# Turning the second layer's x through memory instead of on TensorE

## The chip, the cores and the metric

The kernel runs on one core of a Trainium2 chip. The time is device microseconds (us) of one execution; a comparison uses the median of several. The core's engines are named as in the profile: PE is TensorE (matmul), PEld its weight loads, DVE is VectorE, ACT is ScalarE, POOL is GpSimd, SP is SyncE, which here only issues DMAs. SBUF is the on-chip memory with 128 partitions; PSUM holds the sums of matmuls.

## The reference

Two layers of a decoder trunk, on 256 tokens of width 1024, all in float32. What matters here:

```python
for l in range(DEPTH):                       # DEPTH = 2
    h = rms_norm(x, norm_g[l])               # x * r, r = (mean(x*x) + eps) ** -0.5, times a gain per column
    proj = h @ w_in[l]                       # 1024 -> 10 groups of 512 columns
    q_a, k_a, v_a, q_h, f_h, i_h, q_m, z = jnp.split(proj, split_points, axis=-1)
    ...
    kv_m = rms_norm(mem, mem_norm_g[l]) @ w_mem_kv[l]
    k_m, v_m = jnp.split(kv_m, 2, axis=-1)   # keys are normalised again; cross-attention gives o_m
    ...
    y = jnp.concatenate([o_a, o_h, o_m], axis=-1) * jax.nn.silu(z)
    x = x + y @ w_out[l]
```

## The kernel before

All weights (60 chunks of 128 x 1024 per layer) pass through SBUF once. SyncE loads a chunk into one of four buffers (`wr`). A float32 product is made of three faster ones: each operand is split into a high part (a rounded copy) and a low part (the remainder). For a weight, ScalarE writes the high part (`wh`, line 214, or line 218 where a gain per row is multiplied in) and VectorE the low part (`wl`, lines 228 and 232); there are three buffers of each. TensorE then adds high x high, low x high and high x low into one of four PSUM accumulators of 512 columns (`acc`); four more PSUM tiles (`sd`) serve everything else.

The order of the layer: `group_kv` (line 301; chunks 0 to 7, keys and values of the memory, which don't depend on x), `group_a` twice (line 338; forget gate and query of HGRN2, chunks 8 to 15, which need the whole of hT), then the other groups, then `w_out_phase` (line 1247). Chunks are numbered through: the second layer begins with chunk 60, and its `group_kv` has chunks 60 to 67. `group_kv` takes chunks 0 to 5 with both halves (keys, values), then the key half of 6 and 7, then the value half of both; the key accumulators are copied out by VectorE and ScalarE (`kn`, lines 638 and 639), the value accumulators by `g_vm` (lines 679 and 680).

The work beside the matmuls is written as generators. Each `yield` ends a step, and `slot` (line 263) asks for the next chunks' splits and then lets every active generator do one step. A scheduler orders each engine's instructions by when they become ready and then by this program order; `in_turn` (line 139) fixes an order by hand, `keep_in_program_order` pins an instruction, and `tc.issue_after` puts one behind another on its queue.

`xs` holds x in SBUF, two tiles of 128 rows (tokens). The matmuls need the normalised x as columns: `hT`, 128 partitions x 8 blocks x (high, low) x 256 tokens. `g_norm` (line 468) makes it, in both layers alike:

- ScalarE squares x with a sum (line 473), VectorE makes the mean (line 477), GpSimd the power -0.5 (line 478): r, one number per row;
- VectorE multiplies x by r (line 481), 1024 columns, twice;
- TensorE transposes the 16 blocks of 128 x 128 into PSUM (line 489);
- for each of 8 blocks ScalarE writes the high part with the gain per column, now per partition (line 497), VectorE the low part (line 498).

In the second layer this runs while `group_kv` is on TensorE. x itself is finished in `w_out_phase`, at line 1305, in four additions of 512 columns.

Elsewhere the kernel already turns matrices without TensorE (`across`, line 88): VectorE transposes blocks of 32 x 32 in place (line 95), a DMA stores the result to memory (`there`, line 106), four DMAs load it back with the blocks in their new places (line 111). The keys do this on SyncE's queue, the HGRN output and the attention weights on GpSimd's.

Of the kernel before, what the change touches and what calls it, by code (L numbers as in the profile page):

```python
# [12 lines left out]
F32 = mybir.dt.float32  # L13
# [32 lines left out]
def hymba_kernel(ctx: ExitStack, tc: tile.TileContext, x, mem, mem_t, positions, w_in, w_out, w_mem_kv,  # L46
# [160 lines left out]
    def h_to(n):  # L207
        while st["h"] < min(n, len(chunks)):
            i = st["h"]
            whs[i] = sb.tile([128, 1024], F32R, name="wh", tag="wh", bufs=WH_BUFS)  # L210
            g = chunks[i][2]
            if g is None:
                with behind("ACT"):
                    nc.scalar.copy(whs[i], raws[i])  # L214
            else:
                for sl in parts(i):
                    with behind("ACT"):
                        nc.scalar.activation(whs[i][:, sl], raws[i][:, sl], AF.Copy, scale=gT[:, g:g + 1])  # L218
            st["h"] += 1

    def l_to(n):
# [79 lines left out]
    def group_kv(th, tl, km, vm):  # L301

        acc = [[acc_tile() for _ in range(2)] for _ in range(2)]

        def part(c, g):
            i = c + c0
            wH, wL = whs[i][:, g * 512:(g + 1) * 512], wls[i][:, g * 512:(g + 1) * 512]
            for t in range(2):
                ts = slice(t * 128, (t + 1) * 128)
                mm(acc[g][t], th[:, c, ts], wH, c == 0, False)  # L310
                mm(acc[g][t], tl[:, c, ts], wH, False, False)
                mm(acc[g][t], th[:, c, ts], wL, False, c == 7)

        def fin():
            i = st["c"]
            st["c"] += 1
            del whs[i], wls[i], raws[i]

        c0 = st["c"]
        for c in range(6):  # L320
            for g in range(2):
                part(c, g)
                if g == 1:
                    fin()
                slot(g == 1)
        for c in (6, 7):
            part(c, 0)
            if c == 7:
                spawn(km(acc[0]))
            slot(False)  # L330
        for c in (6, 7):
            part(c, 1)
            fin()
            if c == 7:
                spawn(vm(acc[1]))
            slot(True)
# [116 lines left out]
    def g_mem_r():  # L453
# [11 lines left out]
                                       in1=gT[:, GR_MK:GR_MK + 2], op0=OP.mult, op1=OP.mult)  # L465
        done.add("rm")

    def g_norm(l):
        yield from take("PTh", "PTl")
        xn = [sb.tile([128, D], F32, name="xn", tag=t, bufs=1) for t in ("PTh", "PTl")]  # L470
        ss = small("ssx", 2)
        for t in range(2):
            nc.scalar.activation(xn[t], xs[:, t], AF.Square, accum_out=ss[:, t:t + 1])
        yield 2
        ms = small("msx", 2)
        r = small("rx", 2)
        nc.vector.tensor_scalar(ms, ss, 1.0 / D, EPS, op0=OP.mult, op1=OP.add)
        nc.gpsimd.tensor_tensor(r, ms, pw[:, :2], op=OP.pow)
        yield
        for t in range(2):  # L480
            nc.vector.tensor_scalar(xn[t], xs[:, t], r[:, t:t + 1], None, op0=OP.mult)
        yield 3
        for kp in range(4):
            yield from room("sd")
            pt = side_tile()
            for j in range(2):
                k = kp * 2 + j
                for t in range(2):
                    ins = nc.tensor.transpose(pt[:, j * 256 + t * 128:j * 256 + (t + 1) * 128],  # L489
                                              xn[t][:, k * 128:(k + 1) * 128], ident)  # L490
                    if l == 0:
                        tc.keep_in_program_order(ins)
            for j in range(2):
                k = kp * 2 + j
                c = GR_NORM + 8 * l + k
                src = pt[:, j * 256:(j + 1) * 256]
                nc.scalar.activation(hTh[:, k], src, AF.Copy, scale=gT[:, c:c + 1])
                nc.vector.scalar_tensor_tensor(hTl[:, k], in0=src, scalar=gT[:, c:c + 1],
                                               in1=hTh[:, k].bitcast(F32), op0=OP.mult, op1=OP.subtract)
            rel()  # L500
            if kp % 2 == 1:
                yield
        rel("PTh")
        rel("PTl")
        done.add(f"hT{l}")
# [107 lines left out]
    for tag, n, bufs in (("PTh", 1792, 1), ("PTl", 1792, 1), ("hX", 512, 1), ("qk", 1024, 1), ("sq", 512, 2),  # L613
                         ("vmh", 1024, 1), ("vml", 1024, 1), ("kmh", 1024, 1), ("kml", 1024, 1), ("as", 512, 2),
                         ("al", 256, 2), ("hF", 1024, 1), ("sg", 512, 2), ("ih", 1024, 1),
                         *((f"y{c}{br}", 1024, 1) for br in (H_, A_, M_) for c in "hl"), ("hT1", 512, 1), ("blk", 1536, 1)):
        for _ in range(bufs):
            sb.tile([128, n], F32, name="place", tag=tag, bufs=bufs)

# [15 lines left out]
    def g_km(l, acc):  # L635
        ss = small("ssk", 8)
        kn = sb.tile([128, 2, 512], F32, name="kn", tag="qk", bufs=1)
        nc.vector.tensor_copy(kn[:, 0], acc[0])
        nc.scalar.copy(kn[:, 1], acc[1])  # L639
        yield  # L640
        for t in range(2):
            sumsq(ss[:, t * 4:t * 4 + 4], kn[:, t], 4)
        yield
        while "rm" not in done:
            yield
        ms = small("msk", 8)
        for t in range(2):
            nc.vector.tensor_scalar(ms[:, t * 4:t * 4 + 4], ss[:, t * 4:t * 4 + 4], rm2[:, t:t + 1], EPS,
                                    op0=OP.mult, op1=OP.add)
        r = small("rk", 8)  # L650
        nc.gpsimd.tensor_tensor(r, ms, pw[:, :8], op=OP.pow)
        for t in range(2):
            nc.gpsimd.tensor_scalar(r[:, t * 4:t * 4 + 4], r[:, t * 4:t * 4 + 4], rm[:, t:t + 1], None, op0=OP.mult)
        yield 3
        for t in range(2):
            nc.vector.tensor_tensor(heads(kn[:, t], 4), heads(kn[:, t], 4),
                                    r[:, t * 4:t * 4 + 4][:, :, None].to_broadcast([128, 4, 128]), op=OP.mult)
        yield 3
        kmh = sb.tile([128, 1024], F32R, name="kmh", tag="kmh", bufs=1)
        kt = sb.tile([128, 1024], F32, name="kml", tag="kml", bufs=1)  # L660
        kml = kt.bitcast(F32R)
        g = gkq[:, l:l + 1]
        yield from across(kt.rearrange("p (q r) -> p q r", q=4), kn.rearrange("p t s -> p (t s)"), 8)
        while f"ih{l}" not in done:
            yield
        yield 5
        tc.keep_in_program_order(nc.scalar.activation(kmh, kt, AF.Copy, scale=g))
        tc.keep_in_program_order(nc.vector.scalar_tensor_tensor(kml, in0=kt, scalar=g, in1=kmh.bitcast(F32),
                                                                op0=OP.mult, op1=OP.subtract))
        T["km"] = kmh, kml  # L670
        done.add(f"km{l}")

    def g_vm(l, acc):
        vmh = sb.tile([128, 2, 512], F32R, name="vmh", tag="vmh", bufs=1)
        vml = sb.tile([128, 2, 512], F32R, name="vml", tag="vml", bufs=1)
        while "rm" not in done:
            yield
        for t in range(2):
            nc.scalar.activation(vmh[:, t], acc[t], AF.Copy, scale=rm[:, t:t + 1])
            nc.vector.scalar_tensor_tensor(vml[:, t], in0=acc[t], scalar=rm[:, t:t + 1], in1=vmh[:, t].bitcast(F32),  # L680
                                           op0=OP.mult, op1=OP.subtract)
        T["vm"] = vmh, vml
        yield

# [87 lines left out]

    def y_tiles(br):
        if f"y{br}" not in T:
            T[f"y{br}"] = [sb.tile([128, 4, 256], F32R, name=f"y{c}{br}", tag=f"y{c}{br}", bufs=1) for c in "hl"]
        return T[f"y{br}"]

    def y_store(l, br, u, po):
# [468 lines left out]
    def w_out_phase(l):  # L1247
# [51 lines left out]
        for t in range(2):  # L1299
            for c in range(2):  # L1300
# [4 lines left out]
                nc.vector.tensor_tensor(xv, xv, acc[t][c], op=OP.add)  # L1305
                if last:
                    put(t, c * 512, c * 512 + (256 if split else 512))
                if split:
                    rest = side_tile()
                    both(t, c, 256, 256, last, rest)  # L1310
                    xv = xs[:, t, 768:]
                    nc.vector.tensor_tensor(xv, xv, rest[:, :256], op=OP.add)  # L1312
                    put(t, 768, 1024)
# [11 lines left out]
    for l in range(DEPTH):  # L1325
        group_kv(mTh, mTl, lambda a: g_km(l, a), lambda a: g_vm(l, a))
        need(f"hT{l}")
        group_a(hT, lambda h, a: g_f(l, h, a))
        group_a(hT, lambda h, a: g_q(l, h, a))
        for gen in (lambda l, a: g_qk(l, 1, a), g_ih, lambda l, a: g_qk(l, 0, a), g_zh, g_qm, g_va, A_, M_):  # L1330
            if gen in (A_, M_):
# [53 lines left out]
```

## Time and profile before

| what | value |
| --- | --- |
| median of three runs | 389.35 us (389.11 to 390.02) |
| the profiled execution's own time | 390.01 us |
| its span, first to last instruction | 388.2 us |
| PE / DVE / ACT / POOL busy | 382.4 / 320.5 / 247.6 / 85.3 us |
| second layer's `group_kv`, first to last matmul begun | 195.41 to 218.71 us |
| TensorE's transposes of x in it (16) | from 206.07 us, 1.91 us busy |
| first matmul with the second layer's hT | 219.09 us |

Times inside the execution are counted from the span's start. A line of a timeline has the start, the length, the engine, the line of the kernel, the operation, what it writes and reads, how many were merged, and in brackets the idle time before it with what ended it. A matmul's length is its way through a pipeline; the distance between starts is what it costs. In the lists of groups, the count is followed by the busy time and the mean of one in ns. A DMA line ends with the time from issue to landing.

### The profile page before, as it was taken

To read this page: it belongs to the slowest core of one execution; us is meant where nothing else is said; L and a number is where in the kernel's file an instruction comes from. 1 tells how busy PE (TensorE), PEld (TensorE's weight loads), DVE (VectorE), ACT (ScalarE), POOL (GpSimd) and SP (SyncE) were. 2 spreads that over 40 slices of the span, in tenths; PEclk is the share of its full clock that TensorE was granted. 3 is DMA by queue.
4 is the path that set the end of the run, shared out by engine and by line. 5 is a ranking of instruction groups with operands and counts; after the bars stand their busy time and mean duration, and the time that the engine had idled before them with its cause. 6 is when DMAs were issued, how large, how long until landed. Compare 5 with 4: busy or idle time off the path is not lost.

```text
span 388.2 us, 6790 instructions
## 1 busy us (share of the span) xinstructions
PE 382.4 (98%) x2455; PEld 319.2 (82%) x2455; DVE 320.5 (83%) x621; ACT 247.6 (64%) x414; POOL 85.3 (22%) x129
## 2 busy tenths in 40 slices
PE   7999999999999999999999999999999999999996
PEld 5888888788888888788888888888888889887885
DVE  4789899999659999958577689899696699998663
ACT  5988755567768849754375756445765984785540
POOL 3004400434202623400000040014062054252000
PEclk9999999999999999999999999999999999999999
DMA  8985595439534999985465568736866179999512
GB/s 266 417 307 181 188 320 181 162 113 312 177 108 140 289 289 365 286 258 176 155 210 164 175 206 234 254 110 180 252 191 195 54 255 275 322 335 280 175 39 108
DMA packets 26241, 84.48 MB, mean 218 GB/s; under 512 B 3552, under 2 KB 5984, under 8 KB 26208
## 3 DMA queue, kind: packets, MB, share of 16 engines
q1 hardware_dynamic: 22304, 71.31, 55.7%
q0 software_dynamic: 3616, 12.59, 10.4%
q8 instruction: 19, 0.31, 0.3%
q10 hardware_dynamic: 288, 0.15, 0.1%
q14 instruction: 14, 0.11, 0.1%
HBM read 74.60 MB, written 9.44 MB: 216 GB/s over the span
## 4 chain that ended last, share of the span: by engine, by line
PE 97%; DMA 1%; DVE 0%; SPq 0%; ACT 0%; issue 0%; DVEq 0%
PE acc L276 69%; PE acc L1261 17%; PE sd L276 6%; PE sd L280 4%; DMA wr<-in_w_mem_kv_dram 1%; PE sd L489 1%; PE sd L1017 0%; PE sd L1147 0%; SPq L178 0%; ACT wh L218 0%; DVE xs L1305 0%; DVE xs L1312 0%; DVEq L1312 0%
## 5 line engine op out<-in xcount | busy, mean ns | idle before, releaser
L214 ACT CAST wh<-wr 128x1024 fp32r<-128x1024 f32 x96 | 100.8, 1051 | 68.1 <-PE acc L276 46.8
L228 DVE TENSOR_TENSOR wl<-wr,wh 128x1024 fp32r<-128x1024 f32 x96 | 116.8, 1217 | 26.1 <-ACT wh L214 26.0
L276 PE MATMUL acc<-wh,hT 128*128 128x512 f32 x384 | 122.9, 394 | 0.0
L276 PEld LDWEIGHTS acc<-wh,hT 128*128 128x128 f32 x384 | 71.5, 188 | 15.8 <-issue 0.7
L276 PE MATMUL acc<-wl,hT 128*128 128x512 f32 x192 | 75.6, 394 | 0.0
L276 PE MATMUL acc<-hT,wh 128*128 128x512 f32 x256 | 64.8, 392 | 0.0
L276 PEld LDWEIGHTS acc<-hT,wh 128*128 128x128 f32 x256 | 46.0, 189 | 8.4 <-ACT kn L639 0.4
L276 PEld LDWEIGHTS acc<-wl,hT 128*128 128x128 f32 x192 | 36.1, 188 | 7.3
L1261 PE MATMUL acc<-wh,yl 128*128 128x512 f32 (+1 forms) x96 | 37.2, 387 | 0.0
L1261 PE MATMUL acc<-wl,yh 128*128 128x512 f32 (+1 forms) x96 | 37.2, 387 | 0.0
L232 DVE SCALAR_TENSOR_TENSOR wl<-wr,gT,wh 128x1024 fp32r<-128x1024 f32 (+1 forms) x29 | 31.2, 1096 | 7.1 <-ACT wh L218 7.0
L276 PEld LDWEIGHTS acc<-hT,wl 128*128 128x128 f32 x256 | 34.9, 190 | 2.5
L218 ACT ACTIVATE wh<-wr,gT 128x1024 fp32r<-128x1024 f32 (+1 forms) x29 | 28.3, 1000 | 12.4 <-PE acc L1261 4.1
L276 PE MATMUL acc<-hT,wl 128*128 128x256 f32 x256 | 35.7, 282 | 0.0
L1261 PE MATMUL acc<-wh,yh 128*128 128x512 f32 (+1 forms) x96 | 33.1, 392 | 0.0
L276 PE MATMUL acc<-wh,mTh 128*128 128x512 f32 x64 | 25.3, 399 | 1.2 <-ACT wh L218 0.9
L276 PE MATMUL acc<-wh,mTl 128*128 128x512 f32 x64 | 24.8, 390 | 0.0
L982 POOL TENSOR_TENSOR rka<-msa,pw 128x8 f32<-128x8 f32 x4 | 9.9, 2475 | 58.2 <-DVE msa L981 58.2
L1068 ACT ACTIVATE P<-P,nba,rq 128x128 f32<-128x128 f32 (+1 forms) x32 | 17.1, 537 | 8.3 <-DVE nba L1062 8.3
L1261 PEld LDWEIGHTS acc<-wh,yh 128*128 128x128 f32 x96 | 18.0, 188 | 4.1 <-issue 0.7
L1261 PEld LDWEIGHTS acc<-wh,yl 128*128 128x128 f32 x96 | 18.0, 188 | 3.7
L1261 PEld LDWEIGHTS acc<-wl,yh 128*128 128x128 f32 x96 | 18.0, 188 | 3.5
(219 smaller groups left out, 589.2 us busy)
## 6 DMA issues: line engine op xcount, KB each, us to landing
wr<-in_w_in_dram SPq DMA_DIRECT2D x80, 512.0 KB, 3.7
wr<-in_w_out_dram SPq DMA_DIRECT2D x24, 512.0 KB, 6.0
wr<-in_w_mem_kv_dram SPq DMA_DIRECT2D x15, 512.0 KB, 4.4
there<-blk POOLq DMA_DIRECT2D x4, 768.0 KB, 5.5
PT<-there POOLq DMA_DIRECT2D x16, 192.0 KB, 4.8
there<-blk POOLq DMA_DIRECT2D x6, 512.0 KB, 5.3
there<-blk SPq DMA_DIRECT2D x4, 512.0 KB, 2.9
P<-there POOLq DMA_DIRECT2D x16, 128.0 KB, 6.9
```

What stands on the lines that cost most here:

```text
L214: nc.scalar.copy(whs[i], raws[i])
L218: nc.scalar.activation(whs[i][:, sl], raws[i][:, sl], AF.Copy, scale=gT[:, g:g + 1])
L228: N["wl", i] = nc.vector.tensor_tensor(wls[i], raws[i], whs[i].bitcast(F32), op=OP.subtract)
L232: ins = nc.vector.scalar_tensor_tensor(wls[i][:, sl], in0=raws[i][:, sl], scalar=gT[:, g:g + 1], in1=whs[i][:, sl].bitcast(F32), op0=OP.mu ...
L276: nc.tensor.matmul(o, lhsT=a, rhs=b, start=s, stop=e)
L280: tc.keep_in_program_order(nc.tensor.matmul(o, lhsT=a, rhs=b, start=s, stop=e))
L489: ins = nc.tensor.transpose(pt[:, j * 256 + t * 128:j * 256 + (t + 1) * 128], xn[t][:, k * 128:(k + 1) * 128], ident)
L982: nc.gpsimd.tensor_tensor(r[:, t8], ms[:, t8], pw[:, :8], op=OP.pow)
L1068: nc.scalar.activation(P[:, i, kc[t]], P[:, i, kc[t]], AF.Exp, bias=nb[:, c:c + 1], scale=rq[:, r:r + 1], accum_out=sm[:, c:c + 1])
L1261: ins = nc.tensor.matmul(a, lhsT=y, rhs=wt[:, cs], start=n == (0 if to is None else nk - 2) and j == 0, stop=n == nk - 1 and j == 2)
```

## The change

In the second layer the 16 transposes on TensorE, the multiplication by r beforehand (line 481) and the 16 splits out of PSUM (lines 497 and 498) go. The first layer stays as it is. Instead:

- As soon as a half of x (128 rows) is finished, VectorE turns its 32 x 32 blocks (`x_turn`), not yet normalised, and GpSimd's queue stores it. Both stores are ahead of the loads: four loads for each half are placed behind the power instruction (`T["xr"]`) and behind each other, and bring x back as columns into `xT`, a tile that takes the room of the HGRN branch's y.
- The factor r, one number per row, has become one per column. VectorE copies it over 128 columns (`rc`), and two matmuls with the identity spread it into PSUM (`rb`).
- VectorE multiplies each of 8 column blocks in place by its gain (per partition) and by `rb` (256 columns each). Then ScalarE copies the high parts, four blocks at once, and VectorE subtracts for the low parts (1024 columns each).
- The order on VectorE and on ScalarE around this, from chunk 66 to chunk 70, is fixed with `in_turn`, and the matmuls of chunks 6 and 7 of the second layer's `group_kv` are pinned to program order.

```diff
+        def part(c, g, pinned=False):
...
+                for a, b in ((th, wH), (tl, wH), (th, wL)):
+                    ins = nc.tensor.matmul(acc[g][t], lhsT=a[:, c, ts], rhs=b, start=c == 0 and (a, b) == (th, wH),
+                                           stop=c == 7 and (a, b) == (th, wL))
+                    if pinned:
+                        tc.keep_in_program_order(ins)
...
-            part(c, 0)
+            part(c, 0, c0 > 0)
...
-            part(c, 1)
+            part(c, 1, c0 > 0)
...
+    def x_turned():
+        return sb.tile([128, 8, 256], F32, name="xT", tag=f"y{H_}", bufs=1)
+
+    def x_turn(t):
+        blk = sb.tile([128, 4, 256], F32, name="blk", tag=f"hq{t}", bufs=1)
+        N["xt", t] = nc.vector.transpose(blk.rearrange("p c (n i) -> p c n i", n=8),
+                                         xs[:, t].rearrange("p (n c i) -> p c n i", n=8, c=4))
+        yield
+        there = away.tile([4, 32, 4, 256], F32, name="there", tag="there", bufs=5)
+        T[f"there{t}"] = there
+        T[f"xstore{t}"] = nc.gpsimd.dma_start(there.rearrange("q j c r -> (q j) c r"), blk)
+        done.add(f"xstore{t}")
+        while "xr1" not in done:
+            yield
+        yield 2 + 2 * t
+        for c in range(4):
+            with tc.issue_after(T["xr"].ins):
+                ins = nc.gpsimd.dma_start(T["xT"][c * 32:c * 32 + 32, 4 * t:4 * t + 4],
+                                          there[:, :, c].rearrange("q j r -> j q r"))
+        T["xr"] = ins
+        done.add(f"x{t}moved")
+
+    def g_columns(l, r):
+        xT = T["xT"].rearrange("p q (k i) -> p q k i", i=32)
+        rc = sb.tile([128, 2, 128], F32, name="rc", tag="sq", bufs=2)
+        nc.vector.tensor_copy(rc, r[:, :, None].to_broadcast([128, 2, 128]))
+        yield from reach(l, 4)
+        yield from room("sd")
+        rb = side_tile()
+        for t in range(2):
+            mm_row(rb[:, t * 128:(t + 1) * 128], rc[:, t], ident)
+        rb3 = rb[:, :256].rearrange("p (q i) -> p q i", i=32)
+        while not {"x0moved", "x1moved"} <= done:
+            yield
+        for k in range(8):
+            c = GR_NORM + 8 * l + k
+            N["xT", k] = nc.vector.scalar_tensor_tensor(xT[:, :, k], in0=xT[:, :, k], scalar=gT[:, c:c + 1], in1=rb3,
+                                                        op0=OP.mult, op1=OP.mult)
+        rel()
+        for q in range(2):
+            ks = slice(4 * q, 4 * q + 4)
+            src = xT[:, :, ks].rearrange("p q k i -> p k q i")
+            hi, lo = (a[:, ks].rearrange("p k (q i) -> p k q i", i=32) for a in (hTh, hTl))
+            N["hTh", q] = nc.scalar.copy(hi, src)
+            N["hTl", q] = nc.vector.tensor_tensor(lo, src, hi.bitcast(F32), op=OP.subtract)
+        done.add(f"hT{l}")
...
-        nc.gpsimd.tensor_tensor(r, ms, pw[:, :2], op=OP.pow)
-        yield
+        T["xr"] = nc.gpsimd.tensor_tensor(r, ms, pw[:, :2], op=OP.pow)
+        done.add(f"xr{l}")
+        yield
+        if l:
+            rel("PTh")
+            rel("PTl")
+            yield from g_columns(l, r)
+            return
...
+                elif c:
+                    if t == 0:
+                        T["xT"] = x_turned()
+                    spawn(x_turn(t))
...
+        if l:
+            c = 60 * l
+            in_turn(("wl", c + 6), *(("xT", k) for k in range(4)), ("wl", c + 7), ("hTl", 0),
+                    *(("xT", k) for k in range(4, 8)), ("hTl", 1), ("kn", 0), ("wl", c + 8), ("wl", c + 9), ("vml", 0),
+                    ("vml", 1), ("wl", c + 10))
+            in_turn(("wh", c + 6), ("wh", c + 7), ("hTh", 0), ("wh", c + 8), ("hTh", 1), ("kn", 1), ("wh", c + 9), ("vmh", 0),
+                    ("vmh", 1), ("wh", c + 10))
```

The rest of the diff gives names to the instructions that the two lists use, and puts the two halves of the HGRN branch's y into one tile.

More of the change, by code (lines that the diff above doesn't have):

```diff
@@ L213, in h_to @@
                 with behind("ACT"):
-                    nc.scalar.copy(whs[i], raws[i])
+                    N["wh", i] = nc.scalar.copy(whs[i], raws[i])
             else:
@@ L217, in h_to @@
                     with behind("ACT"):
-                        nc.scalar.activation(whs[i][:, sl], raws[i][:, sl], AF.Copy, scale=gT[:, g:g + 1])
+                        N["wh", i] = nc.scalar.activation(whs[i][:, sl], raws[i][:, sl], AF.Copy, scale=gT[:, g:g + 1])
             st["h"] += 1
@@ L303, in group_kv @@
         acc = [[acc_tile() for _ in range(2)] for _ in range(2)]
-        def part(c, g):
+        def part(c, g, pinned=False):
             i = c + c0
@@ L309, in part @@
                 ts = slice(t * 128, (t + 1) * 128)
-                mm(acc[g][t], th[:, c, ts], wH, c == 0, False)
-                mm(acc[g][t], tl[:, c, ts], wH, False, False)
-                mm(acc[g][t], th[:, c, ts], wL, False, c == 7)
+                for a, b in ((th, wH), (tl, wH), (th, wL)):
[3 more added lines that the diff above has]
+                        tc.keep_in_program_order(ins)
         def fin():
@@ L615, in hymba_kernel @@
                          ("al", 256, 2), ("hF", 1024, 1), ("sg", 512, 2), ("ih", 1024, 1),
-                         *((f"y{c}{br}", 1024, 1) for br in (H_, A_, M_) for c in "hl"), ("hT1", 512, 1), ("blk", 1536, 1)):
+                         (f"y{H_}", 2048, 1), *((f"y{c}{br}", 1024, 1) for br in (A_, M_) for c in "hl"), ("hT1", 512, 1), ("blk", 1536, 1)):
         for _ in range(bufs):
@@ L637, in g_km @@
         kn = sb.tile([128, 2, 512], F32, name="kn", tag="qk", bufs=1)
-        nc.vector.tensor_copy(kn[:, 0], acc[0])
-        nc.scalar.copy(kn[:, 1], acc[1])
+        N["kn", 0] = nc.vector.tensor_copy(kn[:, 0], acc[0])
+        N["kn", 1] = nc.scalar.copy(kn[:, 1], acc[1])
         yield
@@ L678, in g_vm @@
         for t in range(2):
-            nc.scalar.activation(vmh[:, t], acc[t], AF.Copy, scale=rm[:, t:t + 1])
-            nc.vector.scalar_tensor_tensor(vml[:, t], in0=acc[t], scalar=rm[:, t:t + 1], in1=vmh[:, t].bitcast(F32),
-                                           op0=OP.mult, op1=OP.subtract)
+            N["vmh", t] = nc.scalar.activation(vmh[:, t], acc[t], AF.Copy, scale=rm[:, t:t + 1])
+            N["vml", t] = nc.vector.scalar_tensor_tensor(vml[:, t], in0=acc[t], scalar=rm[:, t:t + 1],
+                                                         in1=vmh[:, t].bitcast(F32), op0=OP.mult, op1=OP.subtract)
         T["vm"] = vmh, vml
@@ L774, in y_tiles @@
         if f"y{br}" not in T:
-            T[f"y{br}"] = [sb.tile([128, 4, 256], F32R, name=f"y{c}{br}", tag=f"y{c}{br}", bufs=1) for c in "hl"]
+            if br == H_:
+                y = sb.tile([128, 2, 4, 256], F32R, name=f"y{br}", tag=f"y{br}", bufs=1)
+                T[f"y{br}"] = [y[:, 0], y[:, 1]]
+            else:
+                T[f"y{br}"] = [sb.tile([128, 4, 256], F32R, name=f"y{c}{br}", tag=f"y{c}{br}", bufs=1) for c in "hl"]
         return T[f"y{br}"]
```

## The prediction

> **What bounds the kernel now.** I read the busy table and the chain of waits first.
>
> ```profile
> span 388.2 us, 6790 instructions
> PE 382.4 (98%) x2455; PEld 319.2 (82%) x2455; DVE 320.5 (83%) x621; ACT 247.6 (64%) x414; POOL 85.3 (22%) x129
> PEclk9999999999999999999999999999999999999999
> PE 97%; DMA 1%; DVE 0%; SPq 0%; ACT 0%; issue 0%; DVEq 0%
> ```
>
> TensorE is the bound: 97% of the chain is TensorE behind TensorE, at full granted clock in every slice. So an instruction taken off TensorE is worth its own time, and a hole torn into TensorE costs its own length. Next, the chain in order of time where the second layer begins (columns: start, length, what):
>
> ```profile
> 195.57 10.66 PE acc L276 x47
> 206.23 1.75 PE sd L489 x16
> 207.97 42.39 PE acc L276 x215
> ```
>
> The 16 transposes of x (L489) sit in the middle of the memory-key/value phase, with no idle time on either side: 1.75 us that nothing hides. One 512-column matmul takes 10.66/47 = 0.227 us. The TensorE timeline has the end of that phase and the beginning of the next, the four forget-gate groups that need the whole of hT:
>
> ```profile
> 195.41 0.39 PE L276 MATMUL acc<-wh,mTh 128*128 128x512 f32 x1
> ...
> 218.71 0.39 PE L276 MATMUL acc<-wl,mTh 128*128 128x512 f32 x1
> 219.09 2.14 PE L276 MATMUL acc<-hT,wh 128*128 128x512 f32 x8
> ```
>
> 219.09 us is the time to beat: whatever brings the first hT matmul forward shortens the kernel by as much, because the engine is full from there on.
>
> **What goes from TensorE.** 1.75 us of transposes. In their place come two 128x128 products with the identity that spread the row factors over columns. The nearest row of that shape:
>
> ```profile
> 111.27 1.27 PE L276 MATMUL sd<-ih,hST 128*128 128x128 f32 x10
> 112.38 0.39 PE L276 MATMUL sd<-ih,hX 128*128 128x128 f32 x2
> ```
>
> Ten of them pass between 111.27 and 112.38, 0.11 us each, so two cost 0.22 us. The phase has 96 matmuls (8 chunks, 2 halves, 2 row tiles, 3 products): 195.41 + 96 x 0.227 + 0.22 = 217.4 us is when TensorE could begin on hT. Against 219.09 that is a gain of at most 1.7 us. (Some 0.15 us of it is the wait before 219.09, while an accumulator of the phase was copied out.)
>
> **What must be ready by 217.4.** The new path is turn, store, load, scale, split. I follow the second half of x, the last to be ready. The VectorE timeline:
>
> ```profile
> 192.60 1.28 DVE L1305 TENSOR_TENSOR xs<-xs,acc 128x512 f32<-128x512 f32 x2
> ...
> 195.61 0.69 DVE L1305 TENSOR_TENSOR xs<-xs,acc 128x512 f32<-128x512 f32 x1 [0.67 <-PE acc L1261]
> 196.21 2.47 DVE L232 SCALAR_TENSOR_TENSOR wl<-wr,gT,wh 128x1024 fp32r<-128x1024 f32 x2
> ...
> 200.54 1.41 DVE L481 TENSOR_SCALAR xn<-xs,rx 128x1024 f32<-128x1024 f32 x2
> ```
>
> The residual is whole at 196.3. A turn of 1024 columns takes 1.24 us:
>
> ```profile
> L95 DVE STREAM_TRANSPOSE blk<-zh 128x1024 f32<-128x1024 f32 x2 | 2.5, 1238 | 0.0
> ```
>
> The turn ends at 197.5 if it goes straight behind the addition, at 200.2 if both weight remainders (2.47 us) go first and the first half's turn has pushed the additions back by 0.2 to 0.3. I take 198.75, one remainder ahead, because the second one's operand comes from ScalarE only at 197.17 (194.98 + 2.19), so it need not win the engine:
>
> ```profile
> 194.98 2.19 ACT L218 ACTIVATE wh<-wr,gT 128x1024 fp32r<-128x1024 f32 x2
> ```
>
> The first half is whole at 193.88; its turn and store fall into 193.9 to 196 and end nothing. GpSimd's queue is empty there: its only work between the layers is the row-factor power, which the loads are put behind and which the stores pass.
>
> ```profile
> 198.85 0.72 POOL L478 TENSOR_TENSOR rx<-msx,pw 128x2 f32<-128x2 f32 x1 [35.83 <-DVE msx L477]
> 225.49 2.54 POOL L651 TENSOR_TENSOR rk<-msk,pw 128x8 f32<-128x8 f32 x1 [25.91 <-DVE msk L648]
> ```
>
> Behind the loads, which hold that queue while a store lands, the next instruction is at 225.49: nobody waits for it.
>
> The trip through memory has two kinds of precedent: the key turns on SyncE's queue, and the HGRN output on GpSimd's.
>
> ```profile
> 46.74 0.33 SPq L106 DMA_DIRECT2D there<-blk  x1
> 49.64 1.76 SPq L111 DMA_DIRECT2D kml<-there  x4
> 133.20 0.60 POOL L106 DMA_DIRECT2D there<-blk  x1
> 138.98 2.23 POOL L111 DMA_DIRECT2D zh<-there  x4 [4.79 <-DMA there<-blk]
> zh<-there POOLq DMA_DIRECT2D x8, 128.0 KB, 5.1
> DMA to landing us min/median/max: 3.6/5.1/6.4
> kT<-there SPq DMA_DIRECT2D x8, 128.0 KB, 4.8
> ```
>
> Store to first load is 2.9 us in the one, 5.8 in the other; the fourth load is issued 1.7 us later (3 x 2.23/4), and a load lands after about 5 (3.6 to 6.4 for the HGRN output, least and most). Which store is nearer? The windows (length, busy times of PE, PEld, DVE, ACT, POOL, clock, DMA share, GB/s):
>
> ```profile
> 196.00:200.00 4.00, 4.00 (x20) 3.30 (x19) 3.43 (x5) 3.30 (x5) 0.72 (x1) 1.00 0.37 103
> 200.00:204.00 4.00, 4.00 (x19) 3.32 (x18) 3.14 (x4) 2.29 (x2) 0.00 (x0) 1.00 0.78 290
> 204.00:208.00 4.00, 4.00 (x27) 3.57 (x26) 1.86 (x3) 2.24 (x5) 0.00 (x0) 1.00 0.83 255
> 133.00:139.00 6.00, 6.00 (x40) 5.49 (x40) 6.00 (x14) 1.74 (x4) 1.17 (x4) 1.00 0.94 282
> ```
>
> At 196 to 200 the DMA engines are 37% busy, at 133 to 139 they are 94% busy. The store begins in the first kind of weather, so I take 2.9 plus 0.3 for GpSimd's slower issue (0.60 against 0.33) = 3.2, and for the loads 5.1 plus 0.4 because eight go out, not four, and the weights keep the engines at about 0.8. The last piece of x then lands at 198.75 + 3.2 + 1.7 + 5.5 = 209.15. Bounds: 197.5 + 2.9 + 1.7 + 3.6 = 205.7 and 200.2 + 5.8 + 1.7 + 6.4 = 214.1.
>
> The Trainium skill ("DMA: Bandwidth & Descriptors", section on the anatomy of a DMA on the GpSimd path) gives about 2.0 us plus bytes over 436 GB/s, which makes 3.2 us for a 512 KB store and 2.3 for a 128 KB load. The store rows agree with that; the load rows (4.8 and 5.1) do not, and by the page's figure x would land near 206 and the full 1.7 us be gained.
>
> **From landing to the first matmul.** The order is now written out. Prices:
>
> ```profile
> 209.80 2.04 DVE L498 SCALAR_TENSOR_TENSOR hT<-sd,gT,hT 128x256 fp32r<-128x256 f32 x5
> 211.98 1.28 DVE L232 SCALAR_TENSOR_TENSOR wl<-wr,gT,wh 128x1024 fp32r<-128x1024 f32 x1
> 214.60 1.23 DVE L228 TENSOR_TENSOR wl<-wr,wh 128x1024 fp32r<-128x1024 f32 x1 [1.33 <-ACT wh L214]
> 218.46 0.68 DVE L638 COPY kn<-acc 128x512 f32<-128x512 f32 x1
> 213.51 1.05 ACT L214 CAST wh<-wr 128x1024 fp32r<-128x1024 f32 x1 [1.56 <-PE acc L276]
> 218.45 0.59 ACT L639 COPY kn<-acc 128x512 f32<-128x512 f32 x1 [1.17 <-PE acc L276]
> ```
>
> On VectorE: four column scalings at 2.04/5 = 0.41 (1.64), the remainder of chunk 67 (1.24), the low half of hT's first four (1.22), four more scalings (1.64), then a wait for ScalarE's cast of those (1.05, nothing else in between, since the order is fixed), the second low half (1.22), the copy of the key accumulator (0.68). That is 8.7 us from landing until VectorE has released its accumulator and TensorE can go on; if TensorE needs the ScalarE-copied accumulator first it starts sooner, but the remainder of chunk 68 then comes late, and I count 8.2. I take 8.5, plus 0.2 for hand-overs: 209.15 + 8.7 = 217.85. The gain is 219.09 - 217.85 = **1.24 us**. The profiled execution took 390.01 us (388.2 of span), so its like would be 388.8; from the median of 389.35, which lies 0.66 below the profiled one, it is 388.1.
>
> Break-even follows: hT's path must start by 219.09 - 8.7 = 210.4. Each microsecond later than 208.7 costs a microsecond.
>
> **Waits that the fixed order adds.** Behind the first scaling on VectorE are queued the remainder of chunk 67 and everything to chunk 70. Chunk 67's is needed at 195.41 + 13 x 6 x 0.227 + 0.22 + 0.45 = 213.8, by the third matmul of its first part, which is now pinned; it is done at 209.15 + 2.9 = 212.05, so 1.7 us of cover, gone if x lands after 210.9. VectorE gains two turns, a broadcast copy (0.4, as one scaling) and two 1024-column subtractions (2.48 + 0.4 + 2.44) against 1.41 removed: 3.9 us more, and by the windows it idles 0.6 + 0.9 + 2.1 us of 196 to 208. This holds, but with no room. ScalarE trades eight 256-column casts for two of 1024, which is less.
>
> **Rivals.** (a) *The wait eats the gain*: x lands near 210.4 and hT is as late as before, 389.4. For it: the two unknowns that I took near their good ends (the turn's place, the load's time) have that sum well inside their bounds. Against: a DMA system that is idle in half of 196 to 200.
>
> (b) *Slower: the second store is late and the loads crowd the weights.* The turn waits for both remainders (200.2), the store takes 4.5, halfway between the two precedents, the loads 1.7 + 5.5: landing at 211.9, first hT matmul at 220.6, 1.5 us later than before: 390.9; with the whole 5.8 it is 392.2. It decides from 210.4 on, and is measurable from 211.2. For it: from 200 the engines are at 0.8 already and 1.5 MB of x are added; the stage at 133 to 139 shows what 94% does. The Trainium skill says so too ("DMA: Bandwidth & Descriptors", section on issuing engines not being separate queues): another issuing engine brings no bandwidth, all run on the same 16. Against: weights are fetched ahead, so their slack can give way first.
>
> (c) *Slower, weights late*: x delays two chunks of the phase itself.
>
> ```profile
> wr<-in_w_mem_kv_dram SPq DMA_DIRECT2D x15, 512.0 KB, 4.4
> 202.86 1.15 ACT L218 ACTIVATE wh<-wr,gT 128x1024 fp32r<-128x1024 f32 x1 [1.57 <-PE acc L276]
> ```
>
> A load of 4.4 us stretched to 7 is 2.6 late; ScalarE has 1.57 us to spare before a cast, so about 1 us of hole is left each time, 2.1 for two: 390.2. Against: ScalarE waits there for TensorE, not for a load.
>
> (d) *The change does not do what it says*: TensorE would have waited in those 1.75 us anyway. The chain shows no idle there; it gives 389.4.
>
> **The numbers.** Forecast 388.1 with 0.50 (its own range 387.6 to 388.6); (a) 0.22, (b) 0.20, (c) 0.06, (d) 0.02. About 0.2%, 0.78 us, is what a measurement can tell from none. Faster by more: 0.50; same: 0.22 + 0.02 = 0.24; slower: 0.20 + 0.06 = 0.26. The range reaches from 387.5 (all 1.7 us and a little) to 391.2, past the centre of (b); somewhat under half of (b) and a few per cent below are left out.
>
> **What would show it.** In the profile of after: no L489 transposes near 206; the second half's turn ending near 198.75; the last load of x landing near 209; the first hT matmul near 217.9, and TensorE without a hole before it. A hole of over 1.2 us in front of that matmul, released by VectorE (hT or the copy of the key accumulator), would be (a) or (b); one inside the phase, at chunk 67's remainder or a weight, (b) or (c).

## The result, and the profile after

The change makes the kernel slower: 395.04 us (392.98 to 396.60, five runs) against 389.35, ratio 1.0141 with a 95% interval of 1.0116 to 1.0165. The profiled execution is the slowest of the five, 396.60 us, 6.6 above the profiled one of before.

The page of the changed kernel, its head:

```profile
span 394.8 us, 6779 instructions
PE 383.5 (97%) x2443; PEld 319.9 (81%) x2443; DVE 322.9 (82%) x624; ACT 246.6 (62%) x408; POOL 88.5 (22%) x139
PEclk9999999999999999999999699999999999999999
PE 89%; DMA 6%; DVE 3%; issue 1%; ACT 0%; POOL 0%; SPq 0%; DVEq 0%; ACTq 0%
```

TensorE still reads 97% busy, which tells nothing. The two other lines tell it: one slice of the granted clock (the share of TensorE's full clock, in tenths) has a 6, and the chain, which was TensorE for 97%, now runs for 6% of the span through DMAs. The chain in order of time:

```profile
196.92 1.25 DVE blk L475
198.17 0.39 issue
198.56 7.28 DMA there<-blk
205.84 0.39 issue
...
207.90 8.79 DMA xT<-there
216.96 0.18 DVE xT L506
...
218.61 1.21 DVE wl L232
219.87 6.22 PE acc L311 x16
226.08 33.19 PE acc L276 x176
```

The second half of x is turned where the prediction had it, then takes 7.28 us to be stored and 8.79 for the last load, and VectorE begins the scaling at 216.96. The TensorE timeline has what that does:

```profile
194.89 0.39 PE L311 MATMUL acc<-wh,mTh 128*128 128x512 f32 x1
...
213.25 0.39 PE L311 MATMUL acc<-wh,mTl 128*128 128x512 f32 x1
219.87 0.79 PE L311 MATMUL acc<-wl,mTh 128*128 128x512 f32 x1 [6.22 <-DVE wl L232]
220.46 0.63 PE L311 MATMUL acc<-wh,mTh 128*128 128x512 f32 x1
220.88 0.63 PE L311 MATMUL acc<-wh,mTl 128*128 128x512 f32 x1
...
225.92 3.79 PE L276 MATMUL acc<-hT,wh 128*128 128x512 f32 x16
```

The hole is in front of the third matmul of chunk 67's first part, whose remainder waits on VectorE behind the scaling of x. And behind the hole the matmuls start 0.42 apart (220.46 to 220.88), not 0.227. The windows (length, busy times of PE, PEld, DVE, ACT, POOL, clock, DMA share, GB/s) give the clock and a first sign of what made x late:

```profile
200.00:204.00 4.00, 4.00 (x20) 3.30 (x19) 3.16 (x4) 2.33 (x3) 2.45 (x5) 1.00 0.96 298
204.00:208.00 4.00, 4.00 (x21) 3.40 (x20) 1.12 (x2) 1.15 (x1) 1.75 (x4) 1.00 0.97 285
208.00:212.00 4.00, 4.00 (x19) 3.30 (x19) 0.97 (x1) 1.15 (x1) 0.45 (x1) 1.00 1.06 313
220.00:224.00 4.00, 4.00 (x10) 3.13 (x11) 2.89 (x6) 2.09 (x3) 0.00 (x0) 0.50 0.39 131
```

From 200 to 212 the DMA engines are busy without a pause (0.96 to 1.06, where before had 0.78 and 0.83 up to 208 and 0.29 after it; a transfer counts where it starts, so a window can pass 1) and move only some 300 GB/s. From 220 to 224 the granted clock is 0.50.

From the phase's first matmul to the first one with hT there were 23.68 us before (219.09 - 195.41), now there are 31.03 (225.92 - 194.89). The 7.35 more are: 1.75 of transposes gone, 0.44 of spreading products added, the wait of 0.15 at the end gone; a hole of 6.39 (219.87 less 213.25 + 0.227); and 16 matmuls in 6.05 us instead of 3.63, 2.42 for the clock. The phase begins 0.52 earlier and the rest is 0.23 shorter; that leaves the 6.6 us.

### The profile page after: what moved, and what is told of

Read it like the earlier page. It is cut to its first block, busy times and chain, and to the rows that moved or that the text cites. A ratio compares the mean times of both kernels' runs of the same rounds, so it can differ in the third digit from the quotient of the medians.

```text
span 394.8 us, 6779 instructions
## 1 busy us (share of the span) xinstructions
PE 383.5 (97%) x2443; PEld 319.9 (81%) x2443; DVE 322.9 (82%) x624; ACT 246.6 (62%) x408; POOL 88.5 (22%) x139
## 4 chain that ended last, share of the span: by engine, by line
PE 89%; DMA 6%; DVE 3%; issue 1%; ACT 0%; POOL 0%; SPq 0%; DVEq 0%; ACTq 0%
PE acc L276 56%; PE acc L1320 15%; PE acc L311 6%; PE sd L276 6%; PE sd L280 4%; DMA xT<-there 2%; DMA there<-blk 2%; DMA wr<-in_w_mem_kv_dram 2%; DVE xs L1364 1%; DVE wl L232 1%; DVE blk L475 1%; ACT wh L218 0%; PE sd L1206 0%; PE sd L1076 0%; PE sd L544 0%
## 5 line engine op out<-in xcount | busy, mean ns | idle before, releaser
L311 PE MATMUL acc<-wl,mTh 128*128 128x512 f32 x64 | 21.4, 408 | 6.2 <-DVE wl L232 6.2
L311 PE MATMUL acc<-wh,mTh 128*128 128x512 f32 x64 | 26.5, 417 | 0.4 <-ACT mTh L432 0.3
L311 PE MATMUL acc<-wh,mTl 128*128 128x512 f32 x64 | 25.7, 404 | 0.0
L1320 PE MATMUL acc<-wl,yh 128*128 128x512 f32 (+1 forms) x64 | 24.7, 386 | 0.0
L1320 PE MATMUL acc<-wh,yl 128*128 128x512 f32 (+1 forms) x64 | 24.7, 386 | 0.0
L1041 POOL TENSOR_TENSOR rka<-msa,pw 128x8 f32<-128x8 f32 x4 | 11.3, 2840 | 55.1 <-DVE msa L1040 55.1
L1320 PE MATMUL acc<-wh,yh 128*128 128x512 f32 (+1 forms) x64 | 21.8, 386 | 0.0
L1320 PE MATMUL acc<-wh,y 128*128 128x512 f32 x64 | 20.9, 397 | 0.0
L311 PEld LDWEIGHTS acc<-wl,mTh 128*128 128x128 f32 x64 | 12.5, 196 | 9.3 <-DVE wl L232 6.6
```

The lines of the kernel that those rows point to most:

```text
L311: ins = nc.tensor.matmul(acc[g][t], lhsT=a[:, c, ts], rhs=b, start=c == 0 and (a, b) == (th, wH), stop=c == 7 and (a, b) == (th, wL))
L1041: nc.gpsimd.tensor_tensor(r[:, t8], ms[:, t8], pw[:, :8], op=OP.pow)
L1320: ins = nc.tensor.matmul(a, lhsT=y, rhs=wt[:, cs], start=n == (0 if to is None else nk - 2) and j == 0, stop=n == nk - 1 and j == 2)
```

## The experiments

Two questions: why was x late, and is its lateness the whole loss? The kernel of before was timed again beside these runs, with medians of 389.71 to 389.93, so the ratios are what to compare.

### Without the way through memory

```diff
-        N["xt", t] = nc.vector.transpose(blk.rearrange("p c (n i) -> p c n i", n=8),
+        N["xt", t] = nc.vector.transpose(T["xT"][:, 4 * t:4 * t + 4].rearrange("p c (n i) -> p c n i", n=8),
                                         xs[:, t].rearrange("p (n c i) -> p c n i", n=8, c=4))
         yield
-        there = away.tile([4, 32, 4, 256], F32, name="there", tag="there", bufs=5)
...
-        T["xr"] = ins
         done.add(f"x{t}moved")
```

> Leaves out the way through memory: VectorE turns the blocks of x straight into xT, so the blocks stay on their partitions and the second layer computes with wrongly placed data; the scaling, the splits, the fixed order and the pinned matmuls stay. Theory (the whole loss is the late landing of x, 216.9 where 209.15 was predicted): nothing is late, the first hT matmul comes at about 217 and the kernel gains the 1.5 us of transposes: 387.6 to 388.2. Rival (the fixed order, the extra VectorE work or the pinned matmuls cost by themselves): no faster than before, 389.4 or more.

388.19 us, ratio 0.9955 (0.9932 to 0.9977). The chain:

```profile
195.07 11.11 PE acc L311 x49
206.17 0.44 PE sd L280 x4
206.62 10.67 PE acc L311 x47
217.29 33.19 PE acc L276 x176
```

No hole: 22.2 us from the phase's begin to hT, 1.5 less than before. So the fixed order, VectorE's extra work and the pinned matmuls cost nothing that shows; the loss comes with the trip.

### The weights' remainder ahead of x

```diff
-            in_turn(("wl", c + 6), *(("xT", k) for k in range(4)), ("wl", c + 7), ("hTl", 0),
+            in_turn(("wl", c + 6), ("wl", c + 7), *(("xT", k) for k in range(4)), ("hTl", 0),
```

> On VectorE the remainder of chunk 67 goes ahead of the first four scalings; all else as in the change. Theory (x is late, the order only decides where the hole lies): the phase runs through to about 217, then TensorE waits for hT until x + 7.5 = 224.5; the hole moves and the time falls by 1.5 us at most, 393.5 to 395. Rival (the order tears the hole): no hole over 1.5 us, under 391.

395.26 us, ratio 1.0151 (1.0132 to 1.0169). The TensorE timeline:

```profile
222.90 6.60 PE L276 MATMUL acc<-hT,wh 128*128 128x512 f32 x16 [5.46 <-ACT kn L694]
```

The hole has moved from the phase into its end, 5.46 us, and now the 16 hT matmuls behind it are the slow ones (6.60 us). The order decides where the hole lies and changes its length little. It came out just above the theory's upper edge, since the slow stretch was not saved either. The chain has the scaling's start in this run:

```profile
215.72 1.67 DVE xT L506 x4
```

From there to hT's first matmul are 7.2 us (222.90 - 215.72), and what that matmul waited for was the copy of a key accumulator on ScalarE, not on VectorE.

### Without the two lists of order

```diff
-        if l:
-            c = 60 * l
-            in_turn(("wl", c + 6), *(("xT", k) for k in range(4)), ("wl", c + 7), ("hTl", 0),
...
-                    ("vmh", 1), ("wh", c + 10))
```

> The change without the two written lists of order; x goes by GpSimd's queue in four loads for each half as in the change. Theory (x lands at 215 to 217 and the path from there is 7.5 to 9 us whatever the order): 393.5 to 396. Rival (the lists are what hurts): under 392.

395.20 us, ratio 1.0123 (1.0085 to 1.0161): the same again, so the lists are not what hurts.

### TensorE kept busy in the hole

```diff
         for c in (6, 7):
+            if c == 7 and c0 > 0:
+                pt = side_tile()
+                for _ in range(54):
+                    tc.keep_in_program_order(nc.tensor.matmul(pt[:, :256], lhsT=zb[:, :128], rhs=zb, start=True, stop=True))
+                rel()
             part(c, 0, c0 > 0)
```

> Adds 54 products of zeros (bf16, 256 columns, some 0.11 us each, 5.8 us in all) on TensorE between the key parts of chunks 6 and 7, where the changed kernel has its hole of 6.2 us; nothing else changes. Theory (after the hole TensorE runs at half the granted clock, 0.427 us a matmul instead of 0.227, for 11 matmuls, and that costs time of its own): the matmuls behind the hole pass at 0.227 and the time falls by 1.5 to 2.2 us, to about 393. Rival (the slow stretch is hidden, since hT is ready only at 225 anyway): 395, no change.

394.72 us, ratio 1.0127 (1.0112 to 1.0143), overlapping that of the change. The chain, and the moment of x's landing on VectorE:

```profile
214.24 5.91 PE sd L332 x54
220.15 4.12 PE acc L311 x18
224.27 30.92 PE acc L276 x166
```

```profile
216.63 1.66 DVE L511 SCALAR_TENSOR_TENSOR xT<-xT,gT,sd 128x256 f32<-128x256 f32 x4 [8.04 <-DMA xT<-there]
```

The mechanism is there: with useless work in the hole, the 18 rows behind it take 4.12 us, full speed. The size is not. Between the scaling's start and hT's first matmul in the chain lie 7.6 us here and 9.1 in the change (226.08 - 216.96), 1.5 less, the least that was expected; by the ratios it is some 0.5 (1.0127 against 1.0141), and the intervals overlap. The slow clock takes 2.4 us of TensorE's time, but hT and the accumulators come only just behind. One pair of traces puts 1.5 us of the loss on the clock; over all runs neither that size nor that it costs anything at all is shown. The run is also not quite fair to the theory: the useless work stands ahead of all 18 matmuls, two of which went ahead of the hole in the change, and they begin at 219.91, 0.5 us after the remainder of chunk 67 was ready (219.40).

### One half of x alone

The first half is turned into place as in the first experiment; the second half travels.

```diff
+        if t == 0:
+            N["xt", t] = nc.vector.transpose(T["xT"][:, 0:4].rearrange("p c (n i) -> p c n i", n=8),
+                                             xs[:, t].rearrange("p (n c i) -> p c n i", n=8, c=4))
+            yield
+            done.add("x0moved")
+            return
```

> Only the second half of x travels: the first half is turned straight into xT (wrongly placed, so the result is not the reference's), its store and four loads are gone. Theory (x crowds x: the first half's eight hundred rows and the second store share the engines): the second store lands in 3.5 to 4 us, its loads in 5 to 6, x is there at 208 to 210 and the time is 388 to 389.5. Rival (the weights crowd x): store 6 to 7 and loads 8 as in the change, 393 to 395.

391.58 us, ratio 1.0053 (1.0032 to 1.0075), between the two. VectorE:

```profile
212.61 1.65 DVE L512 SCALAR_TENSOR_TENSOR xT<-xT,gT,sd 128x256 f32<-128x256 f32 x4 [4.94 <-DMA xT<-there]
```

So 4.35 us of the change's lateness (216.96 - 212.61) go with the other half of x; three other runs in which the whole of x travels in the change's form begin the scaling at 214.88 to 216.63, so 2 to 4 us is what can be said. The DMA groups of that stretch:

```profile
there<-blk POOLq DMA_DIRECT2D x1, 512.0 KB, 4.0
xT<-there POOLq DMA_DIRECT2D x4, 128.0 KB, 6.6
```

The store lands in 4.0, not far from the 3.2 predicted, the loads still in 6.6. So both theories fell, each holding half: without the first half the loads are still crowded.

### Fewer weights

```diff
             ap = chunks[i][1]
+            if 64 <= i < 72:
+                raws[i] = raws[i - 4]
+                st["dma"] += 1
+                continue
```

> Leaves out the loads of chunks 64 to 71 (the buffers of four chunks earlier are used again, so the second layer computes with wrong weights); x travels as in the change. With only half of x on the way, x still landed at 212.5, so the other half explains 4 us of the 7.8 of lateness. Theory (the other crowd is the weights): x lands at 207 to 210, no hole over 1 us, 388 to 389.5. Rival (the loads of x are slow by their shape, 1 KB pieces into 32 partitions each, whoever else is there): a load still takes over 6, x lands at 211 to 213 and the time is 390.5 to 392.5.

388.69 us, ratio 0.9970 (0.9951 to 0.9988). The DMA groups of that stretch:

```profile
there<-blk POOLq DMA_DIRECT2D x2, 512.0 KB, 2.9
xT<-there POOLq DMA_DIRECT2D x8, 128.0 KB, 2.9
```

Both halves travel in the change's own form, and with the weights out of the way a store and a load take 2.9 us each, instead of up to 7.3 and 8.8. The rival, slow by shape whoever is there, is out: it takes the crowd.

### One load of 4 KB rows, and the other queue

Two edits, alone and together. The shape: four stores that put the pieces where they belong in memory, then one load of 128 partitions for each half. The rows of 1 KB are not gone by this; they have moved from the loads into the stores.

```diff
-        T[f"xstore{t}"] = nc.gpsimd.dma_start(there.rearrange("q j c r -> (q j) c r"), blk)
+        for q in range(4):
+            T[f"xstore{t}"] = nc.gpsimd.dma_start(there[:, :, q].rearrange("c j r -> j c r"), blk[q * 32:q * 32 + 32])
...
-        for c in range(4):
-            with tc.issue_after(T["xr"].ins):
-                ins = nc.gpsimd.dma_start(T["xT"][c * 32:c * 32 + 32, 4 * t:4 * t + 4],
-                                          there[:, :, c].rearrange("q j r -> j q r"))
+        with tc.issue_after(T["xr"].ins):
+            ins = nc.gpsimd.dma_start(T["xT"][:, 4 * t:4 * t + 4], there.rearrange("c j q r -> (c j) q r"))
```

The queue: `nc.sync` for `nc.gpsimd`, and the loads in line behind the stores instead of behind the power.

> The same bytes on the same queue in another shape: each half is stored in four pieces of 32 partitions (1 KB rows, put where they belong in memory) and loaded by one DMA of 128 partitions with rows of 4 KB. Theory of shape (1 KB pieces into 32 partitions make the loads slow, and four of them are issued one after the other): the load lands in 4 to 5 after its issue and x is there at 207 to 210: 388 to 389.8. Rival (it is bytes that crowd, 2 MB of x beside 2 MB of weights at 300 GB/s): x lands after 213, 392.5 to 396.

> Stores and loads as in the change (four loads of 32 partitions for each half), but on SyncE's queue, as the keys' turn has it. Theory of shape: the loads remain slow, x lands at 212 or later, 391 to 395. Rival (GpSimd's queue loses against SyncE's, which the two key turns with 2.9 for a store speak for): the store lands in 3 to 4, x is there at 208 to 210, 388 to 389.5.

> As the run with one load of 128 partitions for each half, but on SyncE's queue, in one line with the weights. Theory of shape: as there or better by about 1 us, since an issue takes 0.33 instead of 0.55 and no weight that is issued later can go ahead: 387.8 to 389.5. Rival (bytes crowd): weights wait behind the loads of x, which wait for the store; ScalarE waits for chunk 66 or 67 and TensorE has a hole inside the phase: 391 to 396.

| | GpSimd's queue | SyncE's queue |
| --- | --- | --- |
| four loads for a half (the change on the left) | 395.04, 1.0141 (1.0116 to 1.0165) | 393.06, 1.0101 (1.0031 to 1.0170) |
| one load for a half | 391.56, 1.0051 (1.0028 to 1.0073) | 388.47, 0.9965 (0.9950 to 0.9979) |

Neither edit does it alone; together they give the whole gain and beat both kernels. One load on GpSimd's queue lies between its two theories; four loads on SyncE's came out as the theory of shape had it. On GpSimd's queue with one load, the DMA groups and a window:

```profile
there<-blk POOLq DMA_DIRECT2D x8, 128.0 KB, 3.8
xT<-there POOLq DMA_DIRECT2D x2, 512.0 KB, 7.1
208.00:212.00 4.00, 4.00 (x21) 3.40 (x20) 0.00 (x0) 1.15 (x1) 0.00 (x0) 1.00 1.00 406
```

On SyncE's queue with four loads, a weight load out of the chain, the wait of ScalarE, the start of the scaling and a window:

```profile
200.29 7.36 DMA wr<-in_w_mem_kv_dram
```

```profile
ACT wh L218 <- DMA wr<-in_w_mem_kv_dram: 5.1, 2, 4.2
214.38 1.66 DVE L506 SCALAR_TENSOR_TENSOR xT<-xT,gT,sd 128x256 f32<-128x256 f32 x4 [3.88 <-DMA wr<-in_w_in_dram]
208.00:212.00 4.00, 4.00 (x20) 3.30 (x19) 1.28 (x1) 2.30 (x2) 0.00 (x0) 1.00 1.04 278
```

On SyncE's queue with one load: the DMA groups and the issue of the second load, then the windows, then VectorE and TensorE:

```profile
there<-blk SPq DMA_DIRECT2D x8, 128.0 KB, 2.6
xT<-there SPq DMA_DIRECT2D x2, 512.0 KB, 5.9
203.80 0.32 SPq L487 DMA_DIRECT2D xT<-there  x1
```

```profile
204.00:208.00 4.00, 4.00 (x22) 3.36 (x21) 1.91 (x2) 1.24 (x2) 0.00 (x0) 1.00 0.97 374
208.00:212.00 4.00, 4.00 (x19) 3.34 (x18) 2.92 (x6) 1.72 (x2) 0.00 (x0) 1.00 1.01 409
```

```profile
209.74 1.66 DVE L505 SCALAR_TENSOR_TENSOR xT<-xT,gT,sd 128x256 f32<-128x256 f32 x4 [1.08 <-PE acc L311]
217.71 3.79 PE L276 MATMUL acc<-hT,wh 128*128 128x512 f32 x16
```

Equally busy engines move 374 and 409 GB/s where the change had 285 and 313. That goes with the shape and not with the queue: from 208 to 212 it is 406 with one load on GpSimd's queue and 278 with four loads on SyncE's. With rows of 4 KB on the way back, the same crowd is through sooner. A part of it is only moved ahead, since the stores have the small rows now: from 196 to 212, stores and all, the windows add up to 4.6 MB in the change and 5.1 with one load on GpSimd's queue, at about the same busy share.

On SyncE's queue the pieces of the stores take 2.6 where they took 3.8, and the scaling starts at 209.74. Its row names a matmul as what ended the wait, but the spreading product that it reads was through at 207.2; the second load, issued at 203.80 and landed 5.8 later, at 209.6, is what fits. So VectorE still waits for x, but x now comes close to the 209.15 that the prediction had. With four loads on that queue the weights come late (ScalarE waits up to 4.2 us), and x does too: the scaling begins at 214.38, and behind it the remainder of chunk 67 leaves a hole of 3.36 us. Here the row names a weight load, which stands on the same queue; the last load of x, issued at 207.66, took 6.3 us and landed at 214.0. That a queue in line with the weights lets x go first is what I read from this; the issue is also shorter there and stands behind no power instruction, and no run separates these. Why the engines move more in the one shape than in the other stays open too.

### That version without the lists

The same edit as above, on the version with one load on SyncE's queue.

> The version with one load for each half on SyncE's queue, without the two written lists of order (the scheduler orders VectorE and ScalarE; the pinned matmuls stay). Theory (the lists decide little: what counts is when x lands): within 0.8 us of that version, 387.8 to 389.3. Rival (the written order is what lets the path end in time: without it the weights' remainders go ahead of the scaling or behind it at the wrong places): 389.5 to 391.

388.51 us, ratio 0.9958 (0.9938 to 0.9979), no different. When x is there in time, the scheduler's own order is good enough.

## Why the prediction was wrong, step by step

The step that failed is the trip through memory: 3.2 us for the store and 5.5 for the last load, prices of transfers that had met less traffic. In the traffic that the change itself makes they took 7.28 and 8.79. The sentence that a hole in TensorE costs its own length failed too: it left out the clock, though how much that adds stays open. Step by step:

- *What TensorE can save*: right but for a size. The two spreading products take 0.44 us, not 0.22: the row that I divided by ten counts two entries for each float32 product, as the chain without the trip shows (x4 for two). The most to gain was 1.5, not 1.7.
- *The turn of the second half*, one remainder ahead, ending at 198.75: right, 196.92 to 198.17.
- *The store, 3.2*: the step that failed first. 7.28 us measured (5.69 and 4.89 in the second and third experiment, which store in the same form); the first half's took 3.4. I judged the weather by the windows of before, 37% at 196 to 200, and left out the weather that the change itself makes: the first half's loads go out from 200.2, in the middle of the second store, and the weights of the next 3 us besides. At 200 to 204 the share was 0.96.
- *The loads, 1.7 + 5.5*: issue 1.7, right; the last landed 8.79 after its issue. The allowance of 0.4 for eight loads and a share of 0.8 was far too small: 1.5 MB of x came into a stretch that up to 208 had one fifth of its DMA time free, and x and weights together were moved at only some 300 GB/s (3.6 MB in the windows from 200 to 212). A sum of bytes from rows of before would have warned, as an estimate: the same 12 us carried 2.5 MB of weights (290, 255 and 88 GB/s), with x 4.0; at the 282 GB/s of 133 to 139, 0.94 busy, that takes some 14 us, to 214, past the 210.4 of break-even unless the weights give way.
- *Landing at 209.15, at the worst 214.1*: scaling began at 216.96, outside the bounds, since each bound was taken from a transfer that had met less.
- *The path from landing, 8.7*: right as VectorE's sum, 216.96 to 225.45 (224.77 + 0.68 for the key accumulator's copy, the last row of this section), but that is not what hT's first matmul waits for. It began at 225.92, behind the 16 matmuls at the slow clock; in the second experiment it began 7.2 us after the scaling, when ScalarE's copy was done, which the prediction had priced at 8.2. That 8.7 comes close to 225.92 is luck.
- *Chunk 67's cover gone when x lands after 210.9*: right in place. The hole sits there, with VectorE named as I had said a miss would look.
- *Rival (b)*, given 0.20, is what happened: crowding, decided from 210.4 on. Only its first condition did not come: the turn waited for no second remainder. Its price, 390.9 to 392.2, was too low by the later landing and, as far as the slow clock costs, by a term that no rival had.
- *Rival (c)*, weights late, is there as a companion, though it did not end last: the waits of that stretch have ScalarE waiting for two weights of the phase, 5.1 us in all.

```profile
ACT wh L218 <- DMA wr<-in_w_mem_kv_dram: 5.1, 2, 3.0
```

The row of VectorE's release, for the path above:

```profile
224.77 0.68 DVE L693 COPY kn<-acc 128x512 f32<-128x512 f32 x1
```

The chances were a further mistake: the forecast needed the turn, the store and the loads all near their good ends, three unknowns that hang on the same crowd, and I gave it one half.

The two rules of the Trainium skill that the prediction weighed come out thus. The fit in "DMA: Bandwidth & Descriptors" (section on the anatomy of a DMA on the GpSimd path), by which the prediction estimated 3.2 us for a store and 2.3 for a load, comes nearer on an emptier road: with fewer weights 2.9 and 2.9 were measured, with all of them up to 7.3 and 8.8. The prediction says that the store rows agree with it; of its two rows only the 2.9 does, the 5.8 does not. The section on issuing engines not being separate queues spoke against the change and the trace agrees: x and the weights shared the same engines' time, 0.96 to 1.06 of it.

## What to carry to other kernels

A transfer that is moved into a stretch meets the traffic of after, not of before: add its bytes to those that the windows already show, at the rate that this form of transfer reaches, before a landing time is taken from a precedent. Saving TensorE 1.5 us is only worth trying if the replacement is in time when the crowd is counted in; here it took both one wide load for each half and SyncE's queue, and then it did gain 0.35%. A written order cannot mend an operand that is late; it chooses which engine shows it.

## What the runs showed of the hardware that was not expected

A hole in TensorE's work has a second price. After 6.2 us of waiting the matmuls passed 0.43 apart for some 4.5 us, at a granted clock of 0.50; after the 5.46 of the second experiment the 16 matmuls of hT took 6.60 instead of the 3.79 they take elsewhere. How much of this price reaches the kernel's time is what the run with TensorE kept busy leaves open. On SyncE's queue with four loads a hole of 3.36 was followed, a little over 1 us later, by windows at half clock:

```profile
217.00:218.00 1.00, 0.71 (x3) 0.62 (x4) 1.00 (x2) 1.00 (x2) 0.00 (x0) 1.00 0.00 0
219.00:220.00 1.00, 1.00 (x4) 0.76 (x3) 0.94 (x3) 0.02 (x1) 0.00 (x0) 0.50 0.94 377
222.00:223.00 1.00, 1.00 (x6) 0.83 (x5) 1.00 (x3) 1.00 (x3) 0.00 (x0) 1.00 0.00 0
```

Holes of 1.74 us (half of x) and 1.91 (one load, GpSimd's queue) left the clock at 1.00. The clock does not follow the hole directly: by windows of 1 us it fell 4.5 us after the hole had begun in the change, and stayed at half for 6.8; with four loads on SyncE's queue it fell about 1.2 after the hole had ended, and stayed at half for 3.4. The Trainium skill has this rule ("TensorE: Matmul & The Clock Gate", section on the HAM clock gate): an idle window of about 3.4 us halves the clock until a busy one has passed. The runs agree, 3.36 and more against 1.91 and less, and the prediction should have put it into rival (b), whose own figures leave TensorE idle for 3.2 to 4.5 us (220.6 and 1.3 more, against 217.4).

The loads' last microseconds were nearly empty. The DMA rows of the change from 206 to 217, in 40 slices:

```profile
DMA  9999989999998999999999996999962221110000
GB/s 253 343 253 238 238 194 328 402 387 313 283 372 343 402 477 298 238 224 209 268 238 194 224 223 134 223 283 283 268 164 75 74 45 45 60 45 30 30 15 0
```

In the last 2.4 us before x was there, from 214.3 to 216.7, two tenths, then one and then less of the engines' time were in use, at 75 GB/s and below. That would fit a few engines being behind with their share; the trace does not show engines one by one, and most of what started from 213 on were weights (0.36 of 0.42 MB). Which engines, and why, no run here tells.
